# A feed-forward's last product in [token, channel] form, with its norm and residual sum by token

## The chip, the cores and the metric

The kernel runs on one core of a Trainium2 chip. The time is device time in microseconds (us) of one execution; the median of several runs counts. Beside the runs there is one profiled execution, from which all rows of the trace come.

A core has five engines that take their own instructions in order: TensorE (PE, whose weight loads are listed apart as PEld), VectorE (DVE), ScalarE (ACT), GpSimd (POOL) and SyncE (SP), which issues most DMAs. They wait for each other by semaphores.

## The reference

Two transformer blocks run one after the other on 256 tokens of 2048 channels, in float32. The change touches only the last lines of the second block:

```python
def rmsnorm_2(x, w):
    xf = x.astype(jnp.float32)
    r = xf * lax.rsqrt(jnp.mean(xf * xf, axis=-1, keepdims=True) + EPS)
    return (r * w.astype(jnp.float32)).astype(x.dtype)
...
        x = x + rmsnorm_2(mix, norm_mix_post[l])
        h = rmsnorm_2(x, norm_mlp_pre[l])
        ff = jnp.square(jax.nn.relu(h @ w_mlp_in[l])) @ w_mlp_out[l]
        x = x + rmsnorm_2(ff, norm_mlp_post[l])
    return x
```

The inner width is 8192. So `w_mlp_in` is 2048 by 8192 and `w_mlp_out` is 8192 by 2048; `norm_mlp_post` is a gain of 2048 numbers.

## The kernel before

**Layout.** Activations lie as [channel, token]: 128 channels on the partitions, 16 tiles of channels, 256 tokens along a row. `X` is the residual, [128, 16, 256]. A sum over channels is then a sum over partitions, which takes a product with a matrix of ones.

**Products.** Each float32 operand is split into a high and a low part of a shorter type (float32r); hi times hi, hi times lo and lo times hi are summed. `mm` (L277) does one k tile of 128 with two instructions: the weights' high part against hi and lo of the activations at once (512 columns wide, L282 or L284), and the weights' low part against hi (256 wide, L281 or L285). `mm1` (L287) has three instructions 256 wide, which give one summand instead of two. `gemm` (L327) gives a bank of PSUM with 128 channels. `gemm_nat` (L349) exists already and is used for values of the attentions: there the activations are the stationary operand and the weights move, 512 channels wide, so that the result is [token, channel], 128 tokens in each of two banks; a k tile and a half of the tokens take three instructions (L363 to L365).

**The stream of weights.** `order` (L195) lists all weights as chunks of 1024 by 128 numbers. `load` brings two chunks at a time through SP's queue, three such pairs ahead. `Chunk.block` counts the blocks of eight that a chunk has and meanwhile splits a later chunk: the high part on ACT (L258), the low part in two halves on DVE (L267). Three split chunks fit.

**Work beside the products.** Instructions go out in the order in which the program emits them. Whatever is not a product comes from generators, which `slot` moves on once per k tile; the number that a generator yields is the number of slots to its next step. `bank` gives one of four PSUM banks, `free` gives it back.

**The last feed-forward** (L1795 to L1802). Four quarters follow each other; each has 16 tiles of the product with `w_mi`, whose results go through norm, ReLU and square (`relu_gen`) and are split into the operand `A`, and then 16 tiles of the product with `w_mo`, whose results `ff_gen` (L1780) adds into `M2`, [128, 16, 256]. In the last quarter `ff_gen` also squares the finished tile on ACT (`S7.add`, summed in pairs on POOL, L482) and multiplies it with the gain. `post7.sums` (L1666) puts two products with ones into the stream (L1673, L1677), for the sums over the partitions that are ready early; `post7.norm` (L1680) does the last one and gives the factor `R7` as [128, 256], the same on every partition.

**The end** (L1804 to L1845). For three pairs of tiles X is first brought into PSUM by products with the identity (L1811). With the factor known, DVE and POOL multiply `M2` by it (L1814) and add (L1817), or TensorE adds by another product with the identity (L1820) and ACT copies the sum out (L1821). Nine stores go through SP's queue, in the order (0), (1), then pairs 3, 1, 2, 4, 6, 5, 7.

Of the kernel before, what the change touches and what calls it, by code (L numbers as in the profile page):

```python
# [17 lines left out]
T = 256  # L18
# [4 lines left out]
# ---------------------------------------------------------------- constants of the shapes  # L23
# [4 lines left out]
def _consts():  # L28
    """masks and distances, in three groups: used throughout, by the first mixer, by HGRN"""
# [50 lines left out]
def tile_kernel(ctx, tc, a, out, dbg=None):  # L80
# [5 lines left out]
    # ------------------------------------------------------------ pools that live throughout  # L86
# [17 lines left out]
    class Operand:  # L104
        """the [K, T] moving operand of a product, as tiles of 8 k tiles of (hi, lo)"""
# [21 lines left out]
    # ------------------------------------------------------------ activation with a table set  # L127
# [66 lines left out]
    # ------------------------------------------------------------ the stream of weights  # L194
# [36 lines left out]
    def load():  # L231
        """two chunks at a time"""
# [43 lines left out]
    # ------------------------------------------------------------ products  # L276
    def mm(o, h, l, A, start, stop):  # L277
        """o[:, 0:T] += h^T hi, o[:, T:2T] += h^T lo + l^T hi for A = (hi, lo)"""
# [7 lines left out]

    def mm1(o, h, l, A, start, stop):  # L287
        """o += h^T hi + h^T lo + l^T hi"""
        PE.matmul(o, l, A[:, 0], start=start, stop=False)
        PE.matmul(o, h, A[:, 1], start=False, stop=False)  # L290
        PE.matmul(o, h, A[:, 0], start=False, stop=stop)
# [11 lines left out]
    class Chunk:  # L303
        """a chunk of 8 blocks of weights, and the splitting of a later one meanwhile"""
# [22 lines left out]
    def gemm(A, nchunk=2, K0=0, o=None, first=True, last=True, ks=range(8), mm=mm):  # L327
        """a bank with the next nchunk chunks' 128 channels of W^T A, as two summands (mm) or one (mm1)"""
# [12 lines left out]
    def gemm_first(A, n):  # L341
        """n tiles at once, whose chunks come octet by octet"""
# [6 lines left out]
    def gemm_nat(A):  # L349
        """512 channels as [token, channel] in two banks, from 8 chunks of two k tiles"""  # L350
# [18 lines left out]
    def evac(dst, p, R=None, eng=None):  # L369
        """dst = the sum of p's halves (times the norm R)"""  # L370
# [26 lines left out]
    def split(A, k, x, g=None):  # L397
        """A[k] = (hi, lo) of x (times the per-partition g)"""
# [30 lines left out]
    def spread(r):  # L429
        """diagonals of r[token, 2]: ones^T times them is r along the tokens on every partition"""  # L430
# [31 lines left out]
    class Squares:  # L462
        """the sum of the squares of 16 tiles of [128, T]: in S[:, 0] once done, without the last two if apart"""
# [24 lines left out]
    # ------------------------------------------------------------ start: x and its norm  # L488
# [89 lines left out]
    # decay and write strength of the delta rule: columns (head, chunk) of [token in chunk, 16]  # L578
# [66 lines left out]
    # ------------------------------------------------------------ sliding window attention  # L645
# [1303 lines left out]
```

## Time and profile before

| what | us |
|---|---|
| median of 3 runs (2650.56 to 2652.52) | 2651.75 |
| the profiled execution's own span | 2646.6 |
| the four quarters of the last feed-forward, from the first product at 1896.06 to the last at 2626.07 | 730.0 |
| from the start of the last product to the end of the span | 20.5 |

The page lists for each engine the time in which it was busy, and in 40 slices how busy it was. Matmuls are pipelined: the record of one lasts longer than the step to the next, so the step is what a product costs. A row of the timeline has its start, its duration, the engine, the line, the operation, the output and inputs, and in brackets how long the engine had been idle and what ended that. A row of a group has the count, then the busy time and the mean of one in ns, and the idle time before.

### The profile page before, as it was taken

The numbers are of one execution on the slowest core, as the hardware profiler recorded it, in microseconds if no ns is written. First come the engines' busy times: TensorE is split into PE (matmuls) and PEld (weight loads), VectorE is DVE, ScalarE is ACT, GpSimd is POOL, SyncE is SP. The second block draws the span as 40 slices with busy tenths as digits, with TensorE's granted clock in tenths as the row PEclk, the third lists the DMA queues.
The fourth block names the chain that finished last, engine by engine and source line by source line (L and its number), as shares of the span: only waits on it lengthen the run. The fifth ranks groups of instructions, "written<-read, shape, count | busy, mean of one in ns | idle before, by whom it ended". The sixth has DMA issues, their size and how long they took to land.

```text
span 2646.6 us, 40601 instructions
## 1 busy us (share of the span) xinstructions
PE 2588.2 (98%) x15779; PEld 2224.3 (84%) x15779; DVE 1917.6 (72%) x3550; ACT 1366.3 (52%) x2167; POOL 379.7 (14%) x355
## 2 busy tenths in 40 slices
PE   8999999999999999999999999999799999999998
PEld 6888888888888888888888888878688888888886
DVE  7788766667777778888866687976775676666666
ACT  5655545545554565555544454555554443443453
POOL 3112111222321010000001103610300000000001
PEclk9999999999999999999999999999899999999999
DMA  5334435555555545555555554345355555555553
GB/s 208 129 143 142 138 136 189 205 211 186 182 178 187 175 144 191 187 182 188 191 189 181 179 195 148 117 146 198 134 182 187 189 187 187 184 191 188 179 190 112
DMA packets 65857, 460.19 MB, mean 174 GB/s; under 512 B 7296, under 2 KB 7808, under 8 KB 11264
## 3 DMA queue, kind: packets, MB, share of 16 engines
q1 hardware_dynamic: 65088, 456.30, 49.1%
q8 instruction: 123, 2.02, 0.3%
q10 hardware_dynamic: 576, 1.30, 0.1%
q14 instruction: 70, 0.57, 0.1%
HBM read 455.48 MB, written 2.10 MB: 173 GB/s over the span
## 4 chain that ended last, share of the span: by engine, by line
PE 88%; DVE 7%; ACT 3%; issue 1%; POOL 0%; DMA 0%; SPq 0%; ACTq 0%; DVEq 0%; POOLq 0%
PE pg L284 49%; PE pg L285 25%; PE pg L282 3%; DVE wl L267 3%; PE pg L281 2%; PE pn L363 1%; PE pn L364 1%; PE pn L365 1%; ACT wh L258 1%; PE ph L1460 0%; PE pz L754 0%; DMA wr<-in_w_swa_dram 0%; DVE QK L987 0%; ACT L137 0%; DVE Wt L1432 0%
## 5 line engine op out<-in xcount | busy, mean ns | idle before, releaser
L267 DVE TENSOR_TENSOR wl<-wr,wh 128x512 fp32r<-128x512 f32 x1708 | 1228.0, 755 | 234.8 <-ACT wh L258 233.7
L258 ACT ACTIVATE wh<-wr 128x1024 fp32r<-128x1024 f32 x854 | 903.1, 1058 | 884.1 <-PE pg L282 458.6
L284 PE MATMUL pg<-P1a,wh 128*128 128x512 f32 x1360 | 494.6, 402 | 12.8 <-DVE P1a L408 12.8
L284 PE MATMUL pg<-P0b,wh 128*128 128x512 f32 x1287 | 470.7, 402 | 2.0 <-DVE P0b L406 2.0
L284 PE MATMUL pg<-P1b,wh 128*128 128x512 f32 x1188 | 430.5, 399 | 0.0
L285 PE MATMUL pg<-P1a,wl 128*128 128x256 f32 x1360 | 384.2, 282 | 1.6 <-DVE wl L267 1.6
L284 PE MATMUL pg<-P0a,wh 128*128 128x512 f32 x1040 | 383.9, 405 | 0.3 <-DVE P0a L406 0.3
L285 PE MATMUL pg<-P0b,wl 128*128 128x256 f32 x1287 | 361.7, 281 | 1.1 <-DVE wl L267 1.1
L285 PE MATMUL pg<-P1b,wl 128*128 128x256 f32 x1188 | 334.7, 282 | 1.3 <-DVE wl L267 1.3
L284 PEld LDWEIGHTS pg<-P1a,wh 128*128 128x128 f32 x1360 | 258.0, 190 | 68.9 <-issue 10.6
L285 PE MATMUL pg<-P0a,wl 128*128 128x256 f32 x1040 | 293.3, 282 | 0.0
L284 PEld LDWEIGHTS pg<-P0b,wh 128*128 128x128 f32 x1287 | 241.8, 188 | 59.6 <-DVE P0b L406 3.3
L285 PEld LDWEIGHTS pg<-P1a,wl 128*128 128x128 f32 x1360 | 259.8, 191 | 10.5 <-DVE wl L267 2.8
L284 PEld LDWEIGHTS pg<-P1b,wh 128*128 128x128 f32 x1188 | 223.7, 188 | 52.7 <-DVE P1b L408 0.3
L482 POOL TENSOR_TENSOR Sq<-Sq,q 128x512 f32<-128x512 f32 x61 | 90.1, 1476 | 1127.2 <-ACT q L474 1118.7
L285 PEld LDWEIGHTS pg<-P0b,wl 128*128 128x128 f32 x1287 | 242.9, 189 | 3.2 <-DVE wl L267 1.4
L284 PEld LDWEIGHTS pg<-P0a,wh 128*128 128x128 f32 x1040 | 197.1, 190 | 43.0 <-issue 2.0
L285 PEld LDWEIGHTS pg<-P1b,wl 128*128 128x128 f32 x1188 | 225.0, 189 | 4.5 <-DVE wl L267 2.7
L285 PEld LDWEIGHTS pg<-P0a,wl 128*128 128x128 f32 x1040 | 197.9, 190 | 6.4 <-DVE wl L267 0.7
L284 PE MATMUL pg<-P2b,wh 128*128 128x512 f32 x360 | 128.8, 398 | 0.0
L284 PE MATMUL pg<-P2a,wh 128*128 128x512 f32 x352 | 126.3, 398 | 0.0
L285 PE MATMUL pg<-P2b,wl 128*128 128x256 f32 x360 | 100.9, 280 | 0.0
(561 smaller groups left out, 3610.3 us busy)
## 6 DMA issues: line engine op xcount, KB each, us to landing
wr<-in_w_up_dram SPq DMA_DIRECT2D x64, 1024.0 KB, 4.8
wr<-in_w_mi_dram SPq DMA_DIRECT2D x64, 1024.0 KB, 4.8
wr<-in_w_mo_dram SPq DMA_DIRECT2D x64, 1024.0 KB, 4.8
wr<-in_w_gate_dram SPq DMA_DIRECT2D x48, 1024.0 KB, 4.8
wr<-in_w_dn_dram SPq DMA_DIRECT2D x32, 1024.0 KB, 4.8
wr<-in_w_down_dram SPq DMA_DIRECT2D x32, 1024.0 KB, 4.9
wr<-in_w_br_dram SPq DMA_DIRECT2D x16, 1024.0 KB, 4.8
wr<-in_w_o_dram SPq DMA_DIRECT2D x16, 1024.0 KB, 4.8
```

What stands on the lines that cost most here:

```text
L258: S.activation(h, r, AF.Copy)
L267: V.tensor_sub(l[:, s], r[:, s], h[:, s].bitcast(F32))
L281: PE.matmul(o[:, T:2 * T], l, A[:, 0], start=False, stop=False)
L282: PE.matmul(o, h, both, start=False, stop=True)
L284: PE.matmul(o, h, both, start=start, stop=False)
L285: PE.matmul(o[:, T:2 * T], l, A[:, 0], start=False, stop=False)
L363: PE.matmul(ps[t], A[kk][:, 0, cs(t)], hv[:, k], start=s, stop=False)
L364: PE.matmul(ps[t], A[kk][:, 1, cs(t)], hv[:, k], start=False, stop=False)
L365: PE.matmul(ps[t], A[kk][:, 0, cs(t)], lv[:, k], start=False, stop=e)
L482: G.tensor_tensor(self.S, self.S, q, op=ALU.add)
```

## The change

The product with `w_mo` is done by `gemm_nat`: a quarter has four groups of 512 channels, and a group fills two banks, one for each half `c` of the tokens. The weights of `w_mo` are laid out for that before the launch. The sum over the quarters is `MN`, [128 tokens, 2 halves, 2048 channels], in the buffer of `X`. For the residual, `flip_x_gen` transposes `X` during the first quarter's product with `w_mi` (32 transposes on TensorE, eight copies on ACT) into `XT`, in the buffer of `M2`. The gain varies along a row now, so it is loaded repeated on all partitions (`g7`, 1 MB, by SP in the last quarter) and multiplied by DVE. The squares are summed along a row by ACT as it squares (`accum_out`), so the norm's factor is one number per token, and no product with ones and no POOL is used. At the end, for each half: the last group is added and squared, the factor is found by logarithm and exponential and one Newton step on [128, 1], and a total is one DVE instruction (`total`: MN times the factor plus XT) or a product with a diagonal matrix of the factors, on top of XT that is already in PSUM (`total_pe`). The output is stored as [128, 2, 2048], in eight stores.

The diff, without lines in which only comments go:

```diff
-    post7 = Post()
-    S7 = post7.Sq
-    gain7 = W("norm_mlp_post_2")
+    nat = {}
+    ss7 = ec.tile([128, 2, 4], F32, name="ss7")
+    pre7 = ec.tile([128, 2], F32, name="pre7")
...
+    def flip_x_gen():
+        while not all(A2_.ok):
+            yield 1
+        XT = nat["XT"] = cp.tile([128, 2, D], F32, name="XT", tag="P0a")
+        for g in range(4):
+            for c in range(2):
+                ps = pss.tile([128, 4, 128], F32, name="px", tag="s")
+                for j in range(4):
+                    PE.transpose(ps[:, j], X[:, 4 * g + j, cs(c)], ident)
+                yield 1
+                S.copy(XT[:, c, ch(g)], ps.rearrange("p j t -> p (j t)"))
+                yield 11
+        while not S6.done:
+            yield 1
+        nat["MN"] = xc.tile([128, 2, D], F32, name="MN", tag="X")
+
+    def gain_gen():
+        z = ec.tile([128, 4096], F32, name="z7", tag="P2a")
+        nat["G7"], nat["j7"], nat["dg"] = z[:, 0:D], z[:, D:D + 512], z[:, D + 512:D + 768]
+        yield 60
+        nc.sync.dma_start(nat["G7"], a["g7"])
...
+    def ff_gen(q, g, ps):
+        while "MN" not in nat:
+            yield 1
+        for c in range(2):
+            m = nat["MN"][:, c, ch(g)]
+            if q == 0:
+                S.copy(m, ps[c])
+            else:
+                V.tensor_add(m, m, ps[c])
+            free(ps[c])
+            yield 2
+            if q == 3:
+                S.activation(nat["j7"], m, AF.Square, accum_out=ss7[:, c, g:g + 1])
                 yield 2
+                V.tensor_tensor(m, m, nat["G7"][:, ch(g)], op=ALU.mult)
+                yield 2
+        if q == 3 and g == 2:
+            V.tensor_reduce(pre7, ss7[:, :, 0:3], axis=AX.X, op=ALU.add)
+            V.tensor_scalar(pre7, pre7, 1.0 / D, EPS, op0=ALU.mult, op1=ALU.add)
...
-        for n in range(16):
-            spawn(ff_gen(q, n, gemm(A, mm=mm1 if q == 3 and n == 15 else mm)))
+        for g in range(4):
+            ps = gemm_nat(A)
+            if q < 3 or g < 3:
+                spawn(ff_gen(q, g, ps))
...
+    by_pe = ((0, 2), (0, 3), (1, 3))
     sums = {}
+    for b in by_pe:
+        sums[b] = pss.tile([128, 512], F32, name="pf", tag="s")
+        PE.matmul(sums[b], ident, XT[:, b[0], ch(b[1])], start=True, stop=False)
+    x7, y7, t7 = (ec.tile([128, 2], F32, name=n) for n in ("x7", "y7", "t7"))
+    dg7 = nat["dg"].rearrange("p (c t) -> p c t", c=2)
+
+    def last(c):
+        m = MN[:, c, ch(3)]
+        V.tensor_add(m, m, ps[c])
+        S.activation(j7, m, AF.Square, accum_out=ss7[:, c, 3:4])
+
+    def mean(c):
+        V.tensor_scalar(x7[:, c:c + 1], ss7[:, c, 3:4], 1.0 / D, pre7[:, c:c + 1], op0=ALU.mult, op1=ALU.add)
+        act(y7[:, c:c + 1], x7[:, c:c + 1], AF.Ln)
+        act(y7[:, c:c + 1], y7[:, c:c + 1], AF.Exp, scale=-0.5)
+
+    def newton(c):
+        x, y, t = (v[:, c:c + 1] for v in (x7, y7, t7))
+        V.tensor_mul(t, y, y)
+        V.scalar_tensor_tensor(t, t, -0.5, x, op0=ALU.mult, op1=ALU.mult)
+        V.scalar_tensor_tensor(y, t, 1.5, y, op0=ALU.add, op1=ALU.mult)
+        V.tensor_scalar(dg7[:, c], ident, y, None, op0=ALU.mult)
+
+    def gain(c):
+        m = MN[:, c, ch(3)]
+        V.tensor_tensor(m, m, G7[:, ch(3)], op=ALU.mult)
...
+    def total(c, g):
+        o = XT[:, c, ch(g)]
+        V.scalar_tensor_tensor(o, MN[:, c, ch(g)], y7[:, c:c + 1], o, op0=ALU.mult, op1=ALU.add)
+        store(c, g)
+
+    def total_pe(c, g):
+        PE.matmul(sums[c, g], dg7[:, c], MN[:, c, ch(g)], start=False, stop=True)
+        S.copy(XT[:, c, ch(g)], sums[c, g])
+        store(c, g)
+
+    last(0)
+    mean(0)
+    gain(0)
+    newton(0)
+    last(1)
+    mean(1)
+    total(0, 0)
+    gain(1)
+    newton(1)
+    total_pe(0, 2)
+    total_pe(0, 3)
+    total(1, 0)
+    total_pe(1, 3)
+    total(0, 1)
+    total(1, 1)
+    total(1, 2)
...
-    out = nc.dram_tensor("out_0_dram", (128, 16, T), F32, kind="ExternalOutput").ap()
+    out = nc.dram_tensor("out_0_dram", (128, 2, D), F32, kind="ExternalOutput").ap()
```

Of the new functions that the diff calls, `gemm_nat` is unchanged (L349), `ch(g)` is the slice of 512 channels of group g, and `store(c, g)` issues the DMA of one half's group.

More of the change, by code (lines that the diff above doesn't have):

```diff
@@ L1778, in relu_gen @@
         yield from split(A, n, t)
-    def ff_gen(q, n, p):
-        m = M2[:, n]
-        if q == 0:
-            S.copy(m, p[:, T:2 * T])
-            yield 3
-        elif p.shape[1] > T:
-            V.tensor_add(m, m, p[:, T:2 * T])
-        V.tensor_add(m, m, p[:, 0:T])
-        free(p)
-        if q == 3:
-            if n < 15:
-                yield 2
-            yield from S7.add(m)
-            S.activation(m, m, AF.Copy, scale=gain7[:, n:n + 1])
-    spawn(post7.sums())
+    def ff_gen(q, g, ps):
[11 more added lines that the diff above has]
+                S.activation(nat["j7"], m, AF.Square, accum_out=ss7[:, c, g:g + 1])
+                yield 2
+                V.tensor_tensor(m, m, nat["G7"][:, ch(g)], op=ALU.mult)
[3 more added lines that the diff above has]
+            V.tensor_scalar(pre7, pre7, 1.0 / D, EPS, op0=ALU.mult, op1=ALU.add)
+    spawn(flip_x_gen(), 60)
     for q in range(4):
         A = Operand(*octs[q % 2])
+        if q == 3:
+            spawn(gain_gen())
         first = gemm_first(A2_, 3) if q == 0 else []
@@ L1800, in tile_kernel @@
             spawn(relu_gen(A, n, first[n] if n < len(first) else gemm(A2_)))
-        for n in range(16):
-            spawn(ff_gen(q, n, gemm(A, mm=mm1 if q == 3 and n == 15 else mm)))
-    until(lambda: banks["open"] == 0)
-    pairs = [slice(2 * i, 2 * i + 2) for i in range(8)]
-    sums = {}
-    for i in (1, 4, 7):
-        sums[i] = psg.tile([128, 2, T], F32, name="pf", tag="g")
-    for i in (1, 4, 7):
-        if i == 7:
-            R7 = post7.norm()
-        PE.matmul(sums[i], ident, X[:, pairs[i]], start=True, stop=False)
@@ L1813, in times @@
-    def times(eng, v):
-        eng.tensor_tensor(M2[:, v], M2[:, v], bc(R7.unsqueeze(1), [128, v.stop - v.start, T]), op=ALU.mult)
-    def add(eng, v):
-        eng.tensor_tensor(X[:, v], X[:, v], M2[:, v], op=ALU.add)
-    def add_pe(i):
-        PE.matmul(sums[i], ident, M2[:, pairs[i]], start=False, stop=True)
-        S.copy(X[:, pairs[i]], sums[i])
-    def store(v):
-        nc.sync.dma_start(out[:, v], X[:, v])
-    for i in (3, 6):
-        times(G, pairs[i])
-        add(G, pairs[i])
@@ L1829, in tile_kernel @@
-    for v in (slice(0, 1), slice(1, 2)):
-        times(V, v)
-        add(V, v)
-        store(v)
-    times(V, pairs[1])
-    add_pe(1)
-    times(V, pairs[4])
-    add_pe(4)
-    times(V, pairs[2])
-    add(V, pairs[2])
-    times(V, pairs[7])
-    add_pe(7)
-    times(V, pairs[5])
-    add(V, pairs[5])
-    for i in (3, 1, 2, 4, 6, 5, 7):
-        store(pairs[i])
+        for g in range(4):
+            ps = gemm_nat(A)
+            if q < 3 or g < 3:
+                spawn(ff_gen(q, g, ps))
@@ new lines, in tile_kernel @@
+    until(lambda: banks["open"] == 2 and not active)
+    XT, MN, G7, j7 = (nat[k] for k in ("XT", "MN", "G7", "j7"))
+    by_pe = ((0, 2), (0, 3), (1, 3))
+    sums = {}
+    for b in by_pe:
[7 more added lines that the diff above has]
+        S.activation(j7, m, AF.Square, accum_out=ss7[:, c, 3:4])
@@ new lines, in gain, with store @@
+    def gain(c):
+        m = MN[:, c, ch(3)]
+        V.tensor_tensor(m, m, G7[:, ch(3)], op=ALU.mult)
+    def store(c, g):
+        nc.sync.dma_start(out[:, c, ch(g)], XT[:, c, ch(g)])
+    def total(c, g):
[6 more added lines that the diff above has]
+        store(c, g)
@@ L1845, in tile_kernel @@
+    last(0)
[14 more added lines that the diff above has]
+    total(1, 2)
+    for p in ps:
+        free(p)
     drain()
@@ L1911, in layout @@
         o[n] = cat([o[n][by], o[n][len(by):]], 0)
-    o["w_mo"] = i["w_mlp_out_2"][0].reshape(4, 2, 8, 128, 16, 128).transpose(0, 4, 1, 3, 2, 5).reshape(
+    o["w_mo"] = i["w_mlp_out_2"][0].reshape(4, 8, 2, 128, 4, 512).transpose(0, 4, 1, 3, 2, 5).reshape(
         -1, 128, 1024)
+    o["g7"] = np.broadcast_to(i["norm_mlp_post_2"], (128, D))
     v = {}
     for n in ("norm_mix", "norm_xattn", "norm_mem", "norm_ffn", "norm_mix_pre_2", "norm_mix_post_2",
-              "norm_mlp_pre_2", "norm_mlp_post_2", "pool_b_2", "pool_scale_2", "hgrn_norm_w_2", "dn_norm"):
+              "norm_mlp_pre_2", "pool_b_2", "pool_scale_2", "hgrn_norm_w_2", "dn_norm"):
         v[n] = _vec(i[n][0].reshape(-1))
@@ L1947 @@
     got = r.results[0]["out_0_dram"]
-    return np.ascontiguousarray(got.transpose(2, 1, 0).reshape(1, T, D))
+    return np.ascontiguousarray(got.transpose(1, 0, 2).reshape(1, T, D))
```

3 lines of the change are left out of this document (added), and 1 row of the table _VECS.

## The prediction

> **What bounds the kernel now.** I read the head of the page first, then the busy time of each engine by stretches, then the end of the timeline.
>
> ```profile
> span 2646.6 us, 40601 instructions
> PE 2588.2 (98%) x15779; PEld 2224.3 (84%) x15779; DVE 1917.6 (72%) x3550; ACT 1366.3 (52%) x2167; POOL 379.7 (14%) x355
> ```
> ```profile
> 2354.35:2444.59 90.24, 90.24 (x514) 78.53 (x512) 55.83 (x99) 34.58 (x34) 0.00 (x0) 1.00 0.53 187
> 2626.00:2646.60 20.60, 8.19 (x17) 3.37 (x16) 12.14 (x16) 3.57 (x7) 5.55 (x4) 0.79 0.28 102
> ```
>
> The columns of the second fence are the stretch, its length, the busy time of PE, PEld, DVE, ACT and POOL, the granted clock, the DMA share and GB/s. The first stretch is the third quarter of the product with w_mo: TensorE is busy in all 90.24 us of it, at the full clock. The second is the end behind the last product: TensorE works 8.19 of 20.60 us, and DVE 12.14. So two prices count. Whatever the change adds to or takes from TensorE's stream, up to the last product, counts in full; behind it only the chain to the last store counts.
>
> ```profile
> L267 DVE TENSOR_TENSOR wl<-wr,wh 128x512 fp32r<-128x512 f32 x370 | 245.2, 704 | 68.9 <-ACT wh L258 68.9
> L258 ACT ACTIVATE wh<-wr 128x1024 fp32r<-128x1024 f32 x184 | 195.1, 1060 | 279.1 <-PE pg L282 148.7 <-PE pg L284 119.8 <-issue 5.4
> ```
>
> These are the two splits of the weights in the last 546 us. ACT's idle time before a split is ended by TensorE, which frees a buffer, and never by a DMA. So the weights arrive early, and the splitting runs ahead of the products.
>
> **The change, part by part.** First, the product itself. A quarter in the old form is 256 pairs of a 512-wide and a 256-wide product, in the new form 384 products 512 wide; the columns are equal. The trace has both forms: L284 and L285 the old, and L363 to L365 (the function that the change calls) the new.
>
> ```profile
> 2354.35 0.40 PE L284 MATMUL pg<-P0b,wh 128*128 128x512 f32 x1
> ...
> 2444.59 0.39 PE L284 MATMUL pg<-P1a,wh 128*128 128x512 f32 x1
> ```
> ```profile
> 1557.66 0.39 PE L363 MATMUL pn<-wh,P1a 128*128 128x512 f32 x1
> ...
> 1602.23 0.39 PE L365 MATMUL pn<-wl,P1b 128*128 128x512 f32 x1
> ```
>
> The first pair of rows bounds a quarter in the old form: 90.24 us. The second pair is the first and the last of 192 products in the new form in one unbroken run: 44.57 us over 191 steps, 0.2333 us each. 384 of them are 89.6 us. That is 0.64 us less per quarter and **2.6 us less** for four. The less favourable end is a second, short run of the new form:
>
> ```profile
> 1725.04 0.48 PE L363 MATMUL pn<-wh,P1b 128*128 128x512 f32 x1
> ...
> 1732.59 0.39 PE L365 MATMUL pn<-wl,P1b 128*128 128x512 f32 x1
> ```
>
> Its 33 products take 7.55 us over 32 steps, 0.236 us each, because its first one starts behind a pause. At that step a quarter is 90.6 us, and four lose 1.5 us. No row shows the new form faster than 0.2333, so 2.6 us is the other end, and I take it, since the change's runs are long and unbroken.
>
> Second, the sums over the partitions that the old norm puts into the stream (L1673, L1677) go.
>
> ```profile
> 2619.24 0.59 PE L1673 MATMUL pr<-Sq,cst 128*128 128x256 f32 x2
> 2619.48 0.47 PE L281 MATMUL pg<-P2c,wl 128*128 128x256 f32 x1
> 2619.79 0.40 PE L282 MATMUL pg<-P2c,wh 128*128 128x512 f32 x1
> ```
>
> Without the sum L281 would have started at 2619.24 and L282 0.12 later, at 2619.36; it starts at 2619.79, so one sum costs 0.43 us. Two are **0.9 us less**. The last tile's form (L289 to L291) goes too; it is worth some 0.1 us, which I leave out.
>
> Third, X is transposed: 32 transposes in 8 groups of four, inside the first quarter's product with w_mi, where TensorE has no idle time to hide them. The nearest rows are the delta rule's groups of four between two products.
>
> ```profile
> L754 PE MATMUL pz<-cst,kn x16: 270/272/273, 130.5 to 327.4; 128*128 128x128 f32 x16
> ```
> ```profile
> 130.45 0.60 PE L754 MATMUL pz<-cst,kn 128*128 128x128 f32 x4
> 130.81 0.48 PE L284 MATMUL pg<-P0b,wh 128*128 128x512 f32 x1
> 131.13 0.29 PE L285 MATMUL pg<-P0b,wl 128*128 128x256 f32 x1
> ```
>
> From the group's start to L285 0.68 us pass, of which 0.24 are L284's own step. A group costs 0.44 us, and 8 groups cost **3.5 us**. Bounds: 2.9 us at 0.36 a group (if the slower first product behind it is made up), and 8.7 us if the 272 ns that one transpose lasts did not overlap with the next. I take the step, since the rows are the same instruction between the same products. Copying each group out (8 on ACT, 0.58 us each by L1821 below) lies beside the products: ACT is busy 34.58 of 90.24 us in the stretch above, and if it were not hidden it would cost 4.6 us. The gains' load of 1 MB goes into SP's queue in the last quarter, before the weight loads that follow.
>
> ```profile
> wr<-in_w_mo_dram SPq DMA_DIRECT2D x64, 1024.0 KB, 4.8
> ```
>
> A weight load of the same size comes every two chunks (5.6 us), DMA is busy 53% of the time, and by L258's row no split waits for a load. I put it at nothing; without that cover it is one load's landing, 4.8 us.
>
> The new accumulation (512-wide adds on DVE, squares and gains in the last quarter) takes the place of 32 256-wide adds a quarter and of the squares' sums on POOL; it lies beside the products. Each group's two banks have a whole group of time (some 22 us) before TensorE needs them again.
>
> Fourth, the end. Before:
>
> ```profile
> 2626.07 0.28 PE L291 MATMUL pg<-P2c,wh 128*128 128x256 f32 x1
> 2626.19 1.88 PE L1811 MATMUL pf<-X,cst 128*128 128x512 f32 x4
> 2626.39 0.42 DVE L1787 TENSOR_TENSOR M<-M,pg 128x256 f32<-128x256 f32 x1 [5.29 <-PE pg L291]
> ...
> 2628.54 0.47 ACT L142 ACTIVATE g<-pr,eps 128x256 f32<-128x256 f32 x1 [0.74 <-PE pr L1682]
> ...
> 2630.87 0.43 DVE L1814 TENSOR_TENSOR M<-M,g 128x256 f32<-128x256 f32 x1
> ...
> 2631.33 1.36 DVE L1817 TENSOR_TENSOR X<-X,M 128x256 f32<-128x256 f32 x1
> ...
> 2632.72 10.72 SPq L1824 DMA_DIRECT2D out_dram<-X  x9
> ...
> 2637.22 4.83 PE L1820 MATMUL pf<-M,cst 128*128 128x512 f32 x6 [7.86 <-DVE M L1814]
> ...
> 2642.09 0.58 ACT L1821 COPY X<-pf 128x512 f32<-128x512 f32 x1 [0.46 <-PE pf L1820]
> ```
>
> From the start of the last product (2626.07) to the span's end 20.5 us pass. The norm is known at 2630.84; then DVE multiplies and adds apart, and a 256-wide add takes 1.36 us beside POOL where 0.42 is its time alone. The last store is issued by 2643.44, 3.1 us before the end. For the new end I take these rows:
>
> ```profile
> L827 DVE TENSOR_TENSOR dT<-pd,ngc 128x512 f32<-128x512 f32 x4 | 2.7, 687 | 3.2 <-PE pd L826 3.2
> L1611 DVE SCALAR_TENSOR_TENSOR dt<-s,U 128x512 f32<-128x512 f32 x4 | 2.8, 692 | 0.1
> L690 DVE TENSOR_SCALAR mx<-mx,vec 128x2 f32<-128x2 f32 x8 | 1.8, 270 | 0.0
> L388 DVE SCALAR_TENSOR_TENSOR nt<-nt,nx 128x2 f32<-128x2 f32 x7 | 1.1, 161 | 0.2
> L914 DVE TENSOR_SCALAR kdc<-kn,kd 128x128 f32<-128x128 f32 x8 | 1.9, 276 | 0.0
> ```
> ```profile
> L528 ACT ACTIVATE q<-x 128x512 f32<-128x512 f32 x4 | 2.4, 618 | 0.0
> L1524 ACT ACTIVATION_READ_ACCUMULATOR hj<-ho 128x1 f32 x16 | 3.0, 188 | 0.0
> L142 ACT ACTIVATE rc<-nx 128x2 f32<-128x2 f32 x6 | 1.2, 204 | 6.1 <-DVE nx L452 4.1 <-DVE nx L1321 1.9
> ```
> ```profile
> 932.45 0.69 ACT L1236 ACTIVATE Vn<-pn,rc 128x512 f32<-128x512 f32 x1 [0.53 <-PE pn L365]
> 933.85 0.69 ACT L1236 ACTIVATE Vn<-pn,rc 128x512 f32<-128x512 f32 x1 [0.71 <-PE pn L365]
> ```
>
> The last fence shows that the first of the two banks can be read 1.4 us before the second. Let 0 be the start of the last product, 0.03 us each hand-over between instructions. Tokens of half 0: add -0.97 to -0.28 (0.69), square and its sum on ACT to 0.45 (0.62 and 0.19, overlapping by 0.1), mean to 0.72, logarithm and exponential to 1.16, meanwhile DVE's gain to 1.41, three small Newton steps and the diagonal to 2.25. Half 1 stands behind all of it in DVE's order: add to 2.94, square to 3.67, mean to 3.95; total(0,0) to 4.64, gain to 5.33, Newton steps and diagonal to 6.2. Then four totals of 0.69, the last done at 8.9. The three on TensorE run beside it: the identity products end at 2.8, two totals follow by 4.7, the third starts at 6.2; ACT has copied it out by 7.9. SP issues in the written order, so the store of (1,3), at 7.9, holds three finished ones; at some 0.45 us each the last is issued by 9.6. With the 3.1 us of before, the end is at 12.7 instead of 20.5: **7.8 us less**. The lower end comes from what the stores of before moved (GB/s in 40 slices of the last 15 us):
>
> ```profile
> GB/s 0 0 0 0 259 90 0 0 0 0 0 93 279 366 311 0 0 0 0 0 0 0 0 213 404 372 377 60 355 382 399 355 404 377 377 120 0 0 0 0
> ```
>
> At some 380 GB/s the output's 2.1 MB take 5.5 us; with the first store issued at 4.7, 0.85 us to its first packet and 0.9 us of closing, the end is at 11.9 if nothing else limits it. The upper end is 14.6, if the last TensorE total runs at half the clock (0.85 us) and the small operations cost 1 us more.
>
> The half clock comes from the 0.79 of the end's stretch: L1820's six passes take 4.83 us, 0.8 each, where L1811's four take 1.88, 0.43 a step. The new end leaves TensorE idle for 1.5 us at most, against 7.86. The Trainium skill ("TensorE: Matmul & The Clock Gate", Part 1) says that the clock halves after an idle window of about 3.4 us; by that rule the third total runs at full clock, and the trace agrees in so far as 7.86 us of idleness halved it.
>
> **The sum**: -2.6 - 0.9 + 3.5 - 7.8 = -7.8 us. The profiled execution goes from 2646.6 to 2638.8. The median of the runs, 2651.75, lies 5.2 us above that span; I leave this as it is: **2644.0 us**, 0.29% less.
>
> **The rivals.** (1) *The transposes do not overlap.* If each costs its 272 ns, the 32 cost 8.7 us instead of 3.5 and the time is 2649.2: no change. For it: the length of L754's records. Against it: four of them take 0.36 us in the stream. The Trainium skill ("TensorE: Matmul & The Clock Gate", Part 4) gives about 275 ns for a transpose within a kernel, and that such work does not count as activity for the clock; by that price the sum would be an estimate of 2649.3 (32 x 0.275). The step of 0.11 us between L754's records speaks against that price here.
>
> (2) *The end is hardly shorter*: the in-order queues of DVE and SP hold the second half's chain, and it ends at 15 to 17 instead of 12.7. Then 2646.3 to 2648.3, mostly no change. For it: DVE carries some 20 operations of the end in a fixed order, and 0.12 to 0.22 us more for each is enough. Against: POOL is idle, and 0.69 us is what a 512-wide operation takes alone.
>
> (3) *Slower: the chunks' edges.* Each of the 128 chunks brings a new split operand, which the third product of a chunk needs already. If TensorE had to wait for it, it would restart at 0.32 instead of 0.235 us (L284 behind the transposes: 0.085 us more) besides the wait. From (7.8 + 5.3) / 128 = 0.10 us per chunk the kernel is slower; at 0.05 us of waiting and 0.085 of restart it is 128 x 0.135 = 17.3 us, so 2661.3. Against: the run of 192 products crosses 15 such edges and keeps 0.2333 us, and L258 waits for TensorE, not the other way round.
>
> **How the numbers follow.** About 0.2%, 5.3 us, is what a measurement of this kernel can tell from no change; that puts the border at 2646.4. The forecast and its neighbourhood has 0.72, with a range of its own of 2640.5 to 2646.4 (the end at 11.9, 2.9 for the transposes, and 2 us for what the runs scatter; or, upwards, the end at 14.6). Rival 1 has 0.07, rival 2 has 0.14, rival 3 has 0.07. The range runs to 2650.0: it takes in rivals 1 and 2, and the far ends of the unknown costs one at a time (the product's form 2648.1, the copies 2648.6, the gains' load 2648.8).
>
> **What would show it.** Steps of 0.233 us in the new product, 89.6 us a quarter; 0.44 us at each group of transposes; no idle TensorE in front of a new chunk; 12 to 13 us from the start of the last product to the end, POOL without work there, the last operation before the last store a total on DVE. Wrong would be: gaps at the chunks, transposes 0.27 us apart, or a chain behind the last product of 15 us and more.

## The result, and the profile after

| | before | after |
|---|---|---|
| median of 4 runs, us | 2652.14 (2650.56 to 2652.74) | 2633.63 (2631.00 to 2635.03) |
| span of the profiled execution, us | 2646.6 | 2632.9 |

The 4 runs of the kernel before are the three that stand ahead of the prediction and one more. The ratio is 0.9936, with a 95% interval of 0.9924 to 0.9947: the change makes the kernel faster by 0.64%. The forecast was 2644.0 us with a range from 2640.5; the time lies 10.4 us below the forecast and 6.9 us below the range. Sign and most terms were right; one term, the product's, was mis-sized, and a second thing was wrong in the step from the profiled execution's span to the median. The head of the page:

```profile
span 2632.9 us, 39487 instructions
PE 2579.3 (98%) x15277; PEld 2200.2 (84%) x15277; DVE 1880.3 (71%) x3473; ACT 1361.2 (52%) x2153; POOL 364.6 (14%) x344
```

To find the difference, both traces are cut where a quarter's product with `w_mi` or `w_mo` starts. First before (the first quarter with `w_mi`, then the quarters with `w_mo`; the third stands in the prediction), then after (the first quarter with `w_mi`, one with `w_mo`, one with `w_mi`, three more with `w_mo`, the end). The columns are as in the prediction.

```profile
1896.06:1993.04 96.98, 94.42 (x519) 80.92 (x519) 79.06 (x152) 54.00 (x93) 14.43 (x9) 0.96 0.47 163
1993.04:2083.29 90.25, 90.25 (x513) 78.48 (x512) 48.26 (x84) 38.45 (x49) 0.00 (x0) 1.00 0.53 187
2173.69:2263.95 90.26, 90.26 (x514) 78.39 (x512) 55.83 (x99) 34.60 (x34) 0.00 (x0) 1.00 0.54 187
...
2534.99:2626.07 91.08, 91.08 (x533) 79.85 (x532) 59.95 (x95) 45.12 (x62) 9.69 (x7) 1.00 0.43 151
```
```profile
1898.38:1999.02 100.64, 98.10 (x550) 84.58 (x551) 79.06 (x152) 57.71 (x101) 14.11 (x9) 0.96 0.45 157
1999.02:2087.32 88.30, 88.30 (x385) 72.02 (x384) 43.32 (x69) 37.51 (x40) 0.00 (x0) 1.00 0.55 191
2087.32:2177.61 90.29, 90.29 (x513) 78.59 (x512) 62.38 (x124) 45.05 (x64) 0.00 (x0) 1.00 0.53 187
2177.61:2264.66 87.05, 87.05 (x385) 72.10 (x384) 47.21 (x76) 34.63 (x34) 0.00 (x0) 1.00 0.56 193
2354.95:2443.27 88.32, 88.32 (x386) 72.02 (x384) 47.23 (x76) 34.63 (x34) 0.00 (x0) 1.00 0.55 191
2533.56:2620.38 86.82, 86.82 (x384) 71.91 (x383) 48.77 (x80) 36.42 (x45) 0.00 (x0) 1.00 0.46 158
2620.38:2632.90 12.52, 5.81 (x14) 2.19 (x12) 6.88 (x18) 3.69 (x11) 0.00 (x0) 0.92 0.44 168
```

What the reader is to see: TensorE is busy all the time in every quarter with `w_mo`, before and after, so nothing waits at the chunks. But the quarters are not 89.6 us, as forecast. They are 88.3 in two and 87.05 in the other two (the last row ends at the start of the last product, hence 86.82). Summed, the four rows before are 361.83 us and those after 350.49, so 11.3 us less. Taking off the two sums over the partitions (0.9 us, as forecast) leaves 10.4 us (some 0.1 of it for the last tile's form, by the prediction's figure) where the prediction had 2.6.

| term | forecast, us | in the two traces, us |
|---|---|---|
| product with `w_mo` | -2.6 | -10.4 |
| sums over partitions | -0.9 | -0.9 (taken as forecast) |
| transposes (first quarter with `w_mi`) | +3.5 | +3.7 |
| the end: 20.5 to 12.5 | -7.8 | -8.0 |
| other quarters with `w_mi` | 0 | -0.3 |
| everything ahead of 1896 us, which the change doesn't touch | 0 | +2.3 |
| span | -7.8 | -13.7 |

The 2.3 us ahead of 1896 us are no more than two executions of one kernel differ there: the kernel before starts its last feed-forward at 1896.06 in one profile and at 1893.59 in another (`before_again` below), and the changed one at 1898.38 and, with an edit further down only, at 1895.64 (`p2_off32`). One source shows in the granted clock (the third figure from the end of a row). From 770 to 790 us it is 1.00 in the profile before and 0.83 in the one after:

```profile
770.00:790.00 20.00, 17.99 (x99) 1.00 0.49 170
```
```profile
770.00:790.00 20.00, 18.63 (x87) 0.83 0.37 124
```

The transposes stand in the stream as forecast (the first group):

```profile
1924.24 0.60 PE L1786 MATMUL px<-cst,X 128*128 128x128 f32 x4
...
1924.60 0.48 PE L284 MATMUL pg<-P1b,wh 128*128 128x512 f32 x1
...
1924.91 0.29 PE L285 MATMUL pg<-P1b,wl 128*128 128x256 f32 x1
```

From the group's start to L285 0.67 us pass; without L284's own step of 0.23 that is 0.44 for four transposes. And the end runs as it was laid out (the timeline behind the last product, which starts at 2620.38):

```profile
2619.45 0.69 DVE L1854 TENSOR_TENSOR MN<-MN,pn 128x512 f32<-128x512 f32 x1 [4.59 <-PE pn L365]
...
2622.44 0.68 DVE L1854 TENSOR_TENSOR MN<-MN,pn 128x512 f32<-128x512 f32 x1
...
2624.03 0.74 DVE L1878 SCALAR_TENSOR_TENSOR XT<-MN,y,XT 128x512 f32<-128x512 f32 x1
...
2624.81 4.98 SPq L1874 DMA_DIRECT2D out_dram<-XT  x8
2626.07 2.73 DVE L1878 SCALAR_TENSOR_TENSOR XT<-MN,y,XT 128x512 f32<-128x512 f32 x4
2626.21 1.13 PE L1882 MATMUL pf<-MN,z 128*128 128x512 f32 x2 [1.15 <-DVE z L1867]
```

Counted from the last product's start: half 0's add at -0.93 (forecast -0.97), half 1's add at 2.06 (2.25), the first total at 3.65 (3.95), TensorE's third total at 5.83 (6.2), DVE's last total done at 8.42 (8.9), the end at 12.52 (12.7). As forecast, POOL has no work there, and the last operation ahead of the last store is a total on DVE. Whether that total sets the end is tried below.

### The profile page after: what moved, and what is told of

Its sections match the earlier page's. It is cut to its first block, busy times and chain, and to the rows that moved or that the text cites. A ratio compares the mean times of both kernels' runs of the same rounds, so it can differ in the third digit from the quotient of the medians.

```text
span 2632.9 us, 39487 instructions
## 1 busy us (share of the span) xinstructions
PE 2579.3 (98%) x15277; PEld 2200.2 (84%) x15277; DVE 1880.3 (71%) x3473; ACT 1361.2 (52%) x2153; POOL 364.6 (14%) x344
## 4 chain that ended last, share of the span: by engine, by line
PE 87%; DVE 7%; ACT 3%; issue 1%; POOL 1%; DMA 0%; SPq 0%; DVEq 0%; ACTq 0%; POOLq 0%
PE pg L284 41%; PE pg L285 20%; PE pn L363 6%; PE pn L364 6%; PE pn L365 6%; PE pg L282 3%; DVE wl L267 2%; PE pg L281 1%; ACT wh L258 1%; POOL Wt L1438 0%; DVE Wt L1432 0%; PE pz L754 0%; DVE QK L987 0%; ACT L137 0%; ACT L135 0%
## 5 line engine op out<-in xcount | busy, mean ns | idle before, releaser
L284 PE MATMUL pg<-P1a,wh 128*128 128x512 f32 x1360 | 494.4, 401 | 12.8 <-DVE P1a L408 12.8
L284 PE MATMUL pg<-P1b,wh 128*128 128x512 f32 x1188 | 430.3, 399 | 0.4 <-ACT wh L258 0.4
L285 PE MATMUL pg<-P1a,wl 128*128 128x256 f32 x1360 | 383.9, 282 | 1.6 <-DVE wl L267 1.6
L284 PE MATMUL pg<-P0a,wh 128*128 128x512 f32 x1040 | 384.2, 405 | 0.3 <-DVE P0a L406 0.3
L284 PE MATMUL pg<-P0b,wh 128*128 128x512 f32 x1031 | 381.5, 405 | 1.4 <-DVE P0b L406 1.4
L285 PE MATMUL pg<-P1b,wl 128*128 128x256 f32 x1188 | 334.5, 282 | 1.5 <-DVE wl L267 1.4
L284 PEld LDWEIGHTS pg<-P1a,wh 128*128 128x128 f32 x1360 | 257.6, 189 | 68.8 <-issue 10.6
L285 PE MATMUL pg<-P0a,wl 128*128 128x256 f32 x1040 | 293.4, 282 | 0.0
L285 PE MATMUL pg<-P0b,wl 128*128 128x256 f32 x1031 | 290.8, 282 | 1.1 <-DVE wl L267 1.1
L285 PEld LDWEIGHTS pg<-P1a,wl 128*128 128x128 f32 x1360 | 259.4, 191 | 10.5 <-DVE wl L267 2.9
L284 PEld LDWEIGHTS pg<-P1b,wh 128*128 128x128 f32 x1188 | 223.5, 188 | 53.0 <-ACT wh L258 0.7
L284 PEld LDWEIGHTS pg<-P0b,wh 128*128 128x128 f32 x1031 | 194.8, 189 | 49.1 <-DVE P0b L406 2.9
L284 PEld LDWEIGHTS pg<-P0a,wh 128*128 128x128 f32 x1040 | 197.3, 190 | 42.8 <-issue 2.0
L285 PEld LDWEIGHTS pg<-P1b,wl 128*128 128x128 f32 x1188 | 224.7, 189 | 4.8 <-DVE wl L267 3.0
L285 PEld LDWEIGHTS pg<-P0a,wl 128*128 128x128 f32 x1040 | 198.2, 191 | 6.3 <-DVE wl L267 0.7
L285 PEld LDWEIGHTS pg<-P0b,wl 128*128 128x128 f32 x1031 | 195.9, 190 | 1.7 <-DVE wl L267 1.4
L482 POOL TENSOR_TENSOR Sq<-Sq,q 128x512 f32<-128x512 f32 x55 | 81.1, 1475 | 445.1 <-ACT q L474 436.1
L373 DVE TENSOR_TENSOR t<-t,pg 128x256 f32<-128x256 f32 x79 | 32.9, 421 | 90.4 <-ACT t L371 90.3
L1292 POOL TENSOR_TENSOR cv<-cv 128x256 f32<-128x256 f32 x32 | 32.8, 1025 | 333.1 <-DVE cv L1286 333.1
L282 PE MATMUL pg<-P1b,wh 128*128 128x512 f32 x188 | 74.9, 398 | 0.0
```

What stands on the lines that cost most here:

```text
L282: PE.matmul(o, h, both, start=False, stop=True)
L284: PE.matmul(o, h, both, start=start, stop=False)
L285: PE.matmul(o[:, T:2 * T], l, A[:, 0], start=False, stop=False)
L373: V.tensor_add(dst, dst, p[:, 0:T])
L482: G.tensor_tensor(self.S, self.S, q, op=ALU.add)
L1292: G.tensor_tensor(cv[:, 0], cv[:, 0], cv[:, 1], op=ALU.mult)
```

## The experiments

**What sets the step of the new product.** The quarters alternate between two pairs of octets as `A`: P0b and P2a (88.3 us), P2b and P2c (87.05 us). 87.05 us over 384 products are 226.7 ns a step on the P2 octets; with that step for P2a, P0b's is 2 x 88.30 / 384 less 226.7, or 233.2 ns, which is also the step of the rows with P1a and P1b that the prediction used. (P0b's steps below are worked out in the same way.) So the buffer matters. The compiled kernel (the program that the compiler makes of it) says where each lies within a partition: P2a, P2b and P2c start at a multiple of 64 bytes, P0a to P1b 32 bytes off one, the split weights at a multiple of 64. The first theory, H1, is that a stationary operand off a multiple of 64 bytes loads more slowly. Its rival, H2, is that the place or the neighbouring work matters.

`p2_off32`: 32 bytes ahead of the P2 octets.

```diff
     ec = ctx.enter_context(tc.tile_pool(name="ec", bufs=1))
+    ec.tile([128, 8], F32, name="off")
```

> The changed kernel with 32 bytes put in front of the three octets P2a, P2b and P2c, so that all seven octets of the operand A start 32 bytes off a multiple of 64 in their partition (before: only P0a, P0b, P1a and P1b). Theory H1 (a stationary operand that starts 32 bytes off a multiple of 64 costs 6.6 ns more per product): every step of the new product is 233 ns, a quarter of w_mo 89.6 us instead of 87.05 or 88.30; with 4 x 192 + ... products on P2 octets, about +7.7 us, so 2641.3 us. Rival H2 (it is the place of the octet in the memory, or the stage and what runs beside it, not the offset): steps on P2 octets stay at 227 ns, time unchanged at 2633.6 us.

Measured 2640.79 us (2638.61 to 2641.51, 5 runs), ratio to before 0.9959 (0.9946 to 0.9971). Two of its quarters with `w_mo`, on P0b and P2a and on P2b and P2c:

```profile
1995.86:2085.42 89.56, 89.56 (x385) 72.06 (x384) 43.30 (x69) 37.47 (x40) 0.00 (x0) 1.00 0.54 188
...
2175.80:2265.40 89.60, 89.60 (x385) 72.13 (x384) 47.59 (x76) 34.60 (x34) 0.00 (x0) 1.00 0.54 188
```

This is the prediction's 89.6 us to within 0.04, and the whole kernel is 7.2 us slower than the changed one: 32 bytes account for the forecast's error in the product. H2 in the form "the place or the neighbours" falls.

`after_aligned` and `before_aligned`: two small tiles are wider, so that all octets and weights start at multiples of 64 bytes.

```diff
-    vec = cp.tile([128, _VN], F32, name="vec")
+    vec = cp.tile([128, _VN + 8], F32, name="vec")[:, 0:_VN]
-    eps = cp.tile([128, 1], F32, name="eps")
+    eps = cp.tile([128, 16], F32, name="eps")[:, 0:1]
```

> The changed kernel with two small tiles widened so that every octet and every split weight starts at a multiple of 64 bytes. H1: the P0b halves of w_mo go from 233 to 227 ns (-2.6 us over two quarters), and the attentions' products of the same form on P0 and P1 octets (some 48 chunks of 12 products, 6.6 ns each: -3.8 us): about -6.4 us, so 2627.2 us. H2: P0 and P1 octets stay at 233 ns, time unchanged at 2633.6 us.

> The kernel before with the same two tiles widened, everything at multiples of 64 bytes. H1: its w_mo products have the weights as the stationary operand, which were aligned already, so only the attentions' products on P0 and P1 octets gain: -3.8 us, 2648 us; the old product's quarter stays at 90.24 us. H2: no change, 2652 us.

`after_aligned` took 2629.65 us (ratio 0.9916, 0.9903 to 0.993), some 4 us less than the changed kernel and not 6.4; P0b's step went from 233 to 229 ns and not to 227. `before_aligned` took 2649.73 us, ratio 0.9994 (0.9985 to 1.0002). That interval reaches from 4.0 us less to 0.5 us more, so the time alone tells neither from no change nor from H1's 3.8 us. The trace tells more: the run of 192 products that the prediction used starts and ends here with

```profile
1557.51 0.40 PE L363 MATMUL pn<-wh,P1a 128*128 128x512 f32 x1
...
1601.31 0.40 PE L365 MATMUL pn<-wl,P1b 128*128 128x512 f32 x1
```

These are 43.80 us over 191 steps, 229.3 ns each, where it was 233.3. So the steps became shorter here too, but again to 229 and not to 227. H1 had a part of the truth at most.

`w_off32`: only `eps` is widened, so octets and weights are all 32 bytes off.

```diff
-    eps = cp.tile([128, 1], F32, name="eps")
+    eps = cp.tile([128, 16], F32, name="eps")[:, 0:1]
```

> The changed kernel with one small tile widened so that the split weights wh and wl start 32 bytes off a multiple of 64, as do all octets. In the products of the old form the weights are the stationary operand. H1, taken as a rule for any stationary operand (6.6 ns for each of the two weight loads of a k tile): a k tile of the old form takes 366 instead of 353 ns, a quarter of w_mi 93.7 instead of 90.3 us, the new form stays at 233 ns as in p2_off32; over all products of the old form some +70 us, about 2710 us. Rival H2 (only the new form, with the octets as the stationary operand, is sensitive): old form unchanged at 353 ns, all octets 233 ns in the new form, so 2641 us as in p2_off32.

Measured 2628.94 us (2 runs; ratio 0.9918, 0.9899 to 0.9938). Two quarters with `w_mo`:

```profile
1996.23:2083.72 87.49, 87.49 (x385) 72.11 (x384) 43.32 (x69) 37.59 (x40) 0.00 (x0) 1.00 0.57 192
...
2174.07:2261.13 87.06, 87.06 (x386) 72.07 (x384) 47.20 (x76) 34.75 (x34) 0.00 (x0) 1.00 0.56 193
```

Both theories were wrong here: with every operand 32 bytes off, the P2 octets have 227 ns again, P0b 229, and the old product keeps its 353 ns. Alignment by itself is not it. What p2_off32 changed, and w_off32 left as it was for the P2 octets, is the distance between the two operands. The next theory, H3, took this as equal offsets to 128 bytes.

`after_al128`: as after_aligned, with `eps` 32 wide.

> after_aligned left the octet P0b at 229 ns a product beside 227 ns on P2a to P2c. There P0b starts 64 bytes and the weights (the moving operand) 0 bytes off a multiple of 128, while the P2 octets and the weights have the same offset. In this kernel the weights start 64 bytes later, so P0b and they have the same offset, P2a to P2c differ from none of them either; P0b itself lies where it did. Theory H3 (the two operands' offsets to 128 bytes must be equal): P0b 227 ns too, a quarter 87.05 us on either pair of octets; 0.9 us less than after_aligned over two quarters, and about 1 us less in the attentions, so 2627.7 us. Rival H4 (the place of P0b itself counts): P0b stays at 229 ns and a quarter at 87.50 us, so 2629.7 us.

Measured 2626.78 us (ratio 0.9912, 0.9895 to 0.9928). The quarter on P0b and P2a takes 88.15 us; P0b's step is 232.4 ns, so H3 fell, and H4 as well, since P0b had stayed in its place.

```profile
1991.72:2079.87 88.15, 88.15 (x385) 72.22 (x384) 43.34 (x69) 37.50 (x40) 0.00 (x0) 1.00 0.55 191
2079.87:2169.67 89.80, 89.80 (x514) 78.70 (x512) 62.33 (x124) 45.04 (x64) 0.00 (x0) 1.00 0.55 188
```

The second row has something new: the old product with `w_mi` moved too, from 90.3 to 89.8 us.

`probe`: the product alone, behind the changed kernel's last store.

```diff
...
+    def probe(i, off):
+        o = pp[i % 2]
+        for t in range(2):
+            for k in range(2):
+                b = 512 * k + 128 * t + off
+                PE.matmul(o, z[:, b:b + 128], hv[:, k], start=True, stop=True)
+                PE.matmul(o, z[:, b + 256:b + 384], hv[:, k], start=True, stop=True)
+                PE.matmul(o, z[:, b:b + 128], lv[:, k], start=True, stop=True)
...
```

> The changed kernel, and behind its last store, where no other engine works, a measurement of the product by itself: 170 settings of 12 products of the new form, each setting with the octet's columns taken from a place some bytes further on (0 to 60 by 4, 64 to 4128 by 32, then 4384 to 11584 by 288), the weights' place fixed; then the same settings for 4 k tiles of the old form with the activations as the moving operand. H5 (it is the distance between the places of the two operands in the partition that sets the step, in the new form): settings at a distance of 32 modulo 64 give 233 ns, some others 227 ns, with no other engine at work; in the old form 353 ns a k tile at all or nearly all settings. Rival H6 (other engines' reads and writes collide with the operands in some buffers): one step at all settings, 227 ns or less, since nothing else runs. Time: 2633.6 us and some 800 us of probe, so about 3430 us.

The distance is the place in the partition at which the octet starts, less that of the weights. The stretches are eight settings of 12 products each, at distances of 0, 32, 64, 96, 128, 160, 192 and 224 bytes modulo 256; the second number is the stretch's length.

```profile
2878.33:2881.06 2.73, 2.73 (x13) 1.00 0.00 0
2881.06:2883.85 2.79, 2.79 (x13) 1.00 0.00 0
2883.85:2886.65 2.80, 2.80 (x13) 1.00 0.00 0
2886.65:2889.45 2.80, 2.80 (x13) 1.00 0.02 6
2889.45:2892.24 2.79, 2.79 (x14) 1.00 0.00 0
2892.24:2895.04 2.80, 2.80 (x14) 1.00 0.00 0
2895.04:2897.80 2.76, 2.76 (x14) 1.00 0.00 0
2897.80:2900.59 2.79, 2.79 (x13) 1.00 0.00 0
```

Divided by 12, and with the starts read to the ns: 227, 233, 233, 233, 232, 234, 230, 233 ns. This series of eight repeats with a period of 256 bytes over all 11 KB that were probed, while no other engine computed. (The whole run took 3356.43 us, not the some 3430 expected: the probe itself was estimated too long.) So H6 falls and H5 stands: the distance of the two operands modulo 256 bytes sets the step. It also fits each kernel so far; the distances follow from where the tiles lie:

| kernel | distance of P0b, step | distance of P2a, P2b, P2c, step |
|---|---|---|
| after | 224, 233 ns | 0, 227 ns |
| p2_off32 | 224, 233 | 32, 233 |
| after_aligned, w_off32 | 192, 229 | 0, 227 |
| after_al128 | 128, 232 | 0, 227 |

In before_aligned the distance of the attentions' octets is 192, and the step of 229.3 ns fits as well. It is the distance and not the place: the P2 octets that step at 227 ns start at 64, 96, 128 and 192 bytes modulo 256 in these kernels, each time with the weights at the same place.

The old form has a pattern too, and another one. The second half of the probe, at 0, 32, 64, 96, 128, 160, 192, 224 bytes (4 k tiles each; of eight rows the first three and the sixth):

```profile
3243.33:3244.74 1.41, 1.41 (x10) 1.00 0.00 0
3244.74:3246.13 1.39, 1.39 (x10) 1.00 0.00 0
3246.13:3247.52 1.39, 1.39 (x10) 1.00 0.00 0
...
3250.32:3251.71 1.39, 1.39 (x11) 1.00 0.00 0
```

Here the octet is the moving operand, and the distance is again the octet's start less the weights'. A k tile takes 352 ns at 0 and 347 to 348 at 32, 64, 160 and 192; at 96, 128 and 224 it takes 350. H5's "353 ns at nearly all settings" was wrong for this form.

**Using it.** `near_p64`, `near_p32`, `near_p160`: P0 and P2 at 0, P1, the moving operand of `w_mi`, at 64, 32 or 160.

```diff
     P0 = (octet(cp, "P0a"), octet(cp, "P0b"))
+    cp.tile([128, 8], F32, name="pad")
     P1 = (octet(cp, "P1a"), octet(cp, "P1b"))
...
-    eps = cp.tile([128, 1], F32, name="eps")
+    eps = cp.tile([128, 56], F32, name="eps")[:, 0:1]
```

(near_p32; the others have 16 and 48, and 40 and 24, in place of 8 and 56.)

> The changed kernel with a pad between the octets P0 and P1 and a wider small tile before the weights, so that P0a, P0b and P2a to P2c lie at a distance of 0 modulo 256 bytes from the split weights and P1a, P1b at 64. By the probe (H5): new product 227 ns on P0b as on P2, all four quarters of w_mo 87.05 us (now two of 88.30): -2.5 us. If the old product follows the probe in the kernel too (347 ns a k tile at 64, against 353 now): a quarter of w_mi 88.9 instead of 90.3 us, another -5.6 us over four and more in the other stages, about 2624 us or less. Rival (the old product is set by something else in the kernel): w_mi stays at 90.3 us, about 2630 us. H6 (other engines): P0b stays at 233 ns and nothing changes, 2633.6 us.

> As near_p64, with P1a and P1b at a distance of 32 modulo 256 bytes. New product as there (-2.5 us). Old product by the probe: 347 ns a k tile, w_mi 88.9 us. Rival: 90.3 us.

> As near_p64, with P1a and P1b at a distance of 160 modulo 256 bytes. New product as there (-2.5 us). Old product by the probe: 348 ns a k tile, w_mi 89.0 us. Rival: 90.3 us.

Measured 2627.08 us (ratio 0.9915, 0.99 to 0.993), 2614.94 us (0.987, 0.9855 to 0.9884) and 2617.05 us (0.9878, 0.9862 to 0.9895). A quarter with `w_mo` and one with `w_mi` of near_p32, then the one with `w_mi` of near_p64:

```profile
1984.99:2072.07 87.08, 87.08 (x386) 72.07 (x384) 43.39 (x69) 37.51 (x40) 0.00 (x0) 1.00 0.56 193
2072.07:2161.14 89.07, 89.07 (x514) 78.53 (x513) 62.32 (x124) 45.17 (x64) 0.00 (x0) 1.00 0.55 189
```
```profile
2081.87:2171.80 89.93, 89.93 (x514) 78.50 (x512) 62.30 (x124) 45.07 (x64) 0.00 (x0) 1.00 0.55 188
```

The new product follows the probe in all three: 87.03 to 87.08 us in every quarter that is complete. The old product follows it at 32 (89.07 us, by the probe 88.9) and at 160 (88.91), and misses it at 64 (89.93 instead of 88.9), as it does in after_aligned at 192 (90.34 instead of 89.1) and in the changed kernel itself at 224 (90.29 instead of 89.6). What else sets it inside the kernel was not tried. near_p32 is the fastest of all kernels here. By the medians, its two paddings (32 bytes, and an `eps` of 224 bytes) give another 18.7 us; by the differences to the kernel before that ran beside each (34.0 and 18.5 us) it is 15.5. Either way that is about as much as the whole change.

**The transposes.** `no_flip`:

```diff
-                ps = pss.tile([128, 4, 128], F32, name="px", tag="s")
-                for j in range(4):
-                    PE.transpose(ps[:, j], X[:, 4 * g + j, cs(c)], ident)
...
-                S.copy(XT[:, c, ch(g)], ps.rearrange("p j t -> p (j t)"))
+                S.copy(XT[:, c, ch(g)].rearrange("p (j t) -> p j t", j=4), X[:, 4 * g:4 * g + 4, cs(c)])
```

> The changed kernel without the 32 transposes: ACT copies X into XT as it lies, so the transposition of the residual is left out of the computation; everything else stays. The prediction's term (0.44 us for each of 8 groups): -3.5 us, 2630.1 us. Rival 1 (272 ns for each transpose): -8.7 us, 2624.9 us. If other work had hidden them: no change.

Measured 2629.37 us (4 runs; ratio 0.9919, 0.9905 to 0.9932), 4.3 us less than the changed kernel. The stretch with the transposes says it more sharply:

```profile
1898.35:1995.68 97.33, 94.79 (x519) 81.20 (x519) 78.84 (x152) 57.80 (x101) 14.10 (x9) 0.96 0.48 163
```

97.33 us against 100.64 with the transposes: 3.3 us, 0.41 for each of the 8 groups. Single executions differ by some 1 us in this stretch (96.98 in before, 98.12 in before_again), so the second digit isn't firm, but Rival 1's 8.7 us are excluded.

**The end.** `tail_dve`: the three totals of TensorE go to DVE.

```diff
-    by_pe = ((0, 2), (0, 3), (1, 3))
+    by_pe = ()
...
-    total_pe(0, 2)
-    total_pe(0, 3)
+    total(0, 2)
+    total(0, 3)
     total(1, 0)
-    total_pe(1, 3)
+    total(1, 3)
```

> The changed kernel with the three totals of TensorE done by DVE instead (0.69 us each), so DVE has eight totals and TensorE and ACT none; the diagonals are still made. If DVE's order of totals sets the end, as the prediction has it: three totals later, +2.05 us, 14.6 us from the start of the last product to the end. Rival (the stores' transfers set the end): 12.5 us as before. Rival (the end hangs on TensorE's totals): shorter than 12.5 us.

Measured 2633.73 us (2 runs; ratio 0.9937, 0.9917 to 0.9956), in which a us can't be seen; so the trace has to tell. DVE's totals and the stores of tail_dve in the timeline, and its end as a stretch:

```profile
2622.41 6.35 SPq L1874 DMA_DIRECT2D out_dram<-XT  x8
2623.68 4.72 DVE L1878 SCALAR_TENSOR_TENSOR XT<-MN,y,XT 128x512 f32<-128x512 f32 x7
```
```profile
2617.99:2631.44 13.45, 0.39 (x2) 0.00 (x0) 8.87 (x21) 2.06 (x8) 0.00 (x0) 0.61 0.41 156
```

DVE's last total is done 10.41 us behind the last product's start (2628.40 less 2617.99), 1.99 later than in the changed kernel, as expected; the end moved only from 12.52 to 13.45, by 0.93. All three expectations miss: the end moved, but by less than half of what DVE's order would give. So DVE's last total does not set the end of the changed kernel. Its own trace says what does (SPq is SP's issuing of DMAs):

```profile
2627.38 0.59 ACT L1883 COPY XT<-pf 128x512 f32<-128x512 f32 x1 [1.69 <-PE pf L1882]
```
```profile
2627.99 0.33 SPq L1874 DMA_DIRECT2D out_dram<-XT  x1
```

ACT copies TensorE's third total out until 2627.97, and 0.02 us later SP issues its store, that of (1,3). SP had waited 0.8 us for it, while DVE's total (0,1), done at 2627.49, lay ready behind it in SP's order. The last three stores follow 0.43 to 0.48 us apart, so the last issue ends at 2629.79, which is 0.99 us behind DVE's last total (2628.80). In tail_dve every store follows its own total, and the last issue ends 0.36 us behind the last total (2628.76 against 2628.40). That accounts for the 0.93 us: 1.99 for the later totals, less 0.63 for the stores that no longer wait, less 0.43 because the last transfer ends sooner behind its issue (2.68 us from the last issue's end to the end, where it was 3.11). Whether the issues or the transfers pace the last stores of the changed kernel was not tried apart.

**The kernel before, profiled once more.** `before_again`:

> The kernel before, unchanged, for a second profile. If the 5.2 us between the first profile's span and the median of the runs were time outside the span, the profiled time lies 5.2 us above this span too; if they were scatter, this span lies near 2649 us and its own time some 2 us above it.

Its profiled execution had a span of 2645.2 us and took 2647.12 us, 1.9 us more; the median of its 8 runs was 2650.25. So of 5.1 us between that span and the median 1.9 were time outside the span, and 3.1 were scatter. In the 35 executions of the kernel before that ran beside the experiments, spans lay between 2645.5 and 2651.6 us and times 1.8 to 3.1 us above their spans, with a median time of 2649.75. The first profile's span of 2646.6 is among the shorter ones (5 of the 35 are below it), which suggests the same division of its 5.2 us. That isn't shown: the profiled execution's own time is not on record, and the lowest time of its series, 2650.56, is 4.0 us above the span. The stretch from 968 to 978 us in the first profile and in the second shows one source of the scatter:

```profile
968.00:978.00 10.00, 7.74 (x31) 0.66 0.45 173
```
```profile
968.00:978.00 10.00, 9.49 (x46) 0.83 0.39 122
```

The same stretch has a granted clock of 0.66 in one and 0.83 in the other: about 6.8 and 3.4 us of the ten at the half clock, once two and once one equal piece. The Trainium skill ("TensorE: Matmul & The Clock Gate", Part 1) says that the gate's window of 3.4 us runs freely, without starting anew with a kernel, and that the same kernel falls into it differently from run to run; these two rows agree.

## Why the prediction was right and wrong

**The product's form failed, in its size.** The prediction wrote "No row shows the new form faster than 0.2333, so 2.6 us is the other end, and I take it". The sentence is true of the rows, but both runs of rows have P1 octets as the stationary operand, at one and the same distance of 224 bytes from the weights. That made them one sample, not a bound. The changed kernel takes `A` from P0b (224) and P2a to P2c (0), so three quarters of its products step at 227 instead of 233 ns: 384 x 3 x 6.6 ns = 7.6 us, which is nearly the 7.8 us that the term missed. All rows of the new form before the change lie at that distance (P0a and P0b as well), so its trace could not have shown the faster step. p2_off32 puts the P2 octets at a distance of 32 and gets the forecast's 89.6 us a quarter; its 2640.79 us lie 3.2 below the forecast, and that is the next point.

**The median failed, in the offset.** "I leave this as it is" carried all 5.2 us between span and median over to the changed kernel. There the median lies 0.7 us above the profiled span (2633.63 against 2632.9), so 4.5 of the 10.4 us of error lie here. The other 5.9 lie between the spans, 2638.8 forecast and 2632.9 measured: 7.8 for the product, less the 2.3 us of difference ahead of 1896 us, and the rest in small terms. How much of the 5.2 us was scatter is not shown, as said above; what is shown is that the spans of single executions scatter over 6 us. Against the 35 executions the account closes, in part by luck: with the product's term at its measured size the sum is -7.8 - 7.8 = -15.6 us, and 2649.75 less 15.6 is 2634.1, beside the measured 2633.63. Against the runs of before that the result itself is measured by (2652.14) it gives 2636.5, and 2.9 us stay open.

**The transposes were right**: 0.44 us a group in the trace, 3.3 us when they are taken out. The Trainium skill ("TensorE: Matmul & The Clock Gate", Part 4) has about 275 ns for one, and the record's 272 ns agree with that; but their step here is 0.11 us, and it is the step that the stream pays, so the estimate of 2649.3 us by that price doesn't hold here. The copies stayed hidden as well, although the row by which the prediction put them at nothing (ACT busy 34.58 of 90.24 us) is of a quarter with `w_mo`; in the stretch where they fall ACT was busy 54.00 of 96.98 us, and TensorE is idle there for 2.5 us with the copies as without.

**The end was right**, at 12.52 us against 12.7, by a sum of some twenty steps each a little too long. Its last step, the store of (1,3) that holds the finished ones behind it in SP's order, was forecast at 7.9 us and came at 7.61 (2627.99 less 2620.38). So by the trace TensorE's third total and SP's order lead to the end, as the sum has it. What tail_dve's expectation made of this, that DVE's order of totals sets the end, was wrong: DVE's last total has some 0.6 us to spare. TensorE's third total ran at the full clock, behind 1.15 us of idleness, as the prediction took it: the granted clock is 1.00 from 2626.21 to 2627.34.

**The rivals.** Rival 1 is excluded by no_flip, rival 2 (15 to 17 us) by the end's 12.52 us. Rival 3, a stop at each chunk, is excluded by the quarters: in 87.05 us 384 products follow each other with no idle time, over 32 chunks. The gains' load stayed hidden as costed: TensorE is busy throughout.

## What to carry to other kernels

When a duration is taken from another place of a kernel, note which buffers its operands lie in: rows that share one buffer are one sample, and "no row shows it faster" is no bound. In a kernel that TensorE bounds, try a few paddings between the stationary and the moving operands; here some bytes were worth 0.6 to 0.7%. And set a forecast against several executions' spans, or widen it by their scatter (6 us here), since one profiled execution can be among the luckiest.

## What the runs showed of the hardware

The step between two products with float32r operands, 512 columns wide, depends on the distance of the stationary from the moving operand within a partition, with a period of 256 bytes: 227 ns at 0, 230 at 192, 232 to 234 at the other multiples of 32. It needs no other engine's traffic (probe), and near_p32, near_p64 and near_p160 show it in whole kernels. The pair of a 512-wide and a 256-wide product, whose weights and activations change roles, has its worst of these at 0 (352 ns) and its best at 32 (347) in the probe; inside the kernels it kept to the probe within 1.3 ns at 0, 32, 128 and 160, and not at 64, 192 and 224. Distances of 4 to 28 bytes, one setting each, gave 231 to 235 ns for the first and 345 to 357 for the second. Why the distance matters no run here shows.
